# The last quarter of x on ScalarE's load queue, and 36 warm-up products instead of 39

## The chip, the cores and the metric

The kernel runs on one core of one Trainium2 chip. A core has five engines, which each run their own list of instructions: TensorE (PE, with its weight loads as PEld), VectorE (DVE), ScalarE (ACT), GpSimd (POOL) and SyncE (SP). They wait for each other, and for loads from memory (DMA), by semaphores. The metric is the device time of one execution in microseconds (us), lower is better.

## The reference

Two blocks of a hybrid transformer, on 256 latent tokens and 256 context tokens of width 1024. Every sublayer has this form, where `mod` comes from the condition `c` by a product with `mod_w`:

```python
def _rms(t, g):
    y = t32 * lax.rsqrt(jnp.mean(t32 * t32, axis=-1, keepdims=True) + NORM_EPS)
    return y.astype(t.dtype) * g

def _modulate(t, g, shift, scale):
    return _rms(t, g) * (1 + scale) + shift

lat = lat + 0.5 * mod[:, 0, 2] * _swiglu(_modulate(lat, norm_g[i, 0], mod[:, 0, 0], mod[:, 0, 1]), ffn_w13[i, 0], ffn_w2[i, 0])
```

Block 0 is a feed-forward layer, a short convolution and a second feed-forward layer, on both streams; block 1 has attention with two key heads in the middle and leaves the latent stream alone at its end. What concerns the change is the very first step: the root mean square over the 1024 channels of the input, for 512 tokens.

## The kernel before

The tokens of both streams stand side by side: `x` is one tile of 128 partitions by 8 channel groups by 512 tokens (256 latent, 256 context), 2 MB in all. Weights come in pieces of 512 KB, and each is split into a rounded part (`wh`, ScalarE, line 108) and the rest (`wl`, VectorE, line 109); a product is made of three products of such parts (lines 137 to 139). The loads of `x` and of nearly all weights are issued by SP, the constants by ScalarE's queue.

The start, with the lines of the profile:

```python
    def cload(key, shape, eng=None):                                    # 72
        t = const.tile(list(shape), F32, name=key, tag=key)
        (eng or nc.scalar).dma_start(t, a[key])                         # 74
        return t

    ccol = cload("ccol", [P, KT, 2])                                    # 78
    x = act.tile([P, KT, T2], F32, name="x", tag="x")
    for q in range(4):
        nc.sync.dma_start(x[:, 2 * q : 2 * q + 2, :], a["xT"][:, 2 * q : 2 * q + 2, :])   # 81
    modb = cload("modb", [P, 2, 72])                                    # 82
    normg = cload("normg", [P, 2, 3, KT])
    ident = cload("ident", [P, P])
```

After that ScalarE makes SiLU of the condition (`sccol`, line 96, from `ccol`) and issues the small load `rowsum`. Then the first stage runs:

- `square_add(k)` for k = 0 to 7, in that order: ScalarE squares channel group k of `x` (`sq`, line 258, out of three buffers in turn); VectorE copies (line 264, k = 0) or adds (line 266, k = 1 to 6) the two halves into `acc`, one for the latent tokens and one for the context tokens. The last square goes to TensorE as it is. One quarter of `x` holds two channel groups.
- `sb1` (line 904): VectorE adds 1 to a part of `modb`. In VectorE's list it stands ahead of the first copy into `acc`.
- `fill(WARM)` (line 897): TensorE multiplies a tile of ones by itself, 39 times, into a tile `idle` that nothing reads. Each such product is two records of the profile.
- `rms_sum` (line 275): TensorE sums `acc` and the last square over the partitions into `ss`; ScalarE takes the root (`rs`, line 280) and VectorE the reciprocal (`ri`, line 284); two products with `ident` (line 293) spread it over all partitions (`ris`, line 953).
- `mod_pe` and `mod_turn` (steps P and T): rows of the modulation, `pr`, from `pm` (loads at line 916) and `sccol` at line 926, turned by products with `rowsum` at line 938, and added to `sb1` or `modb` at line 943.
- `hr` (line 963) and `hh`, `hl` (lines 973 to 987): the normalized input, on which the first products with `w13` wait (line 1000, `pg` and `pu`).

The order within this stage is written out by hand (`FIRST_STEPS`, under a manual schedule for TensorE, VectorE, ScalarE and SP); elsewhere a scheduler orders the instructions when the program is built. Landings are told by eight semaphores that the loads take in turn: a load that takes a semaphore waits, on the engine that issues it, until the load before it on that semaphore has landed.

Of the kernel before, what the change touches and what calls it, by code (L numbers as in the profile page):

```python
# [9 lines left out]
F32 = mybir.dt.float32  # L10
# [6 lines left out]
P = 128  # L17
D = 1024
KT = D // P
S = 256  # L20
T2 = 2 * S
# [6 lines left out]
HEADS = 8  # L28
KVH = 2
EPS = 1e-6  # L30
WARM = 39
FILL = 5


# [13 lines left out]
def hybrid_kernel(ctx: ExitStack, tc: tile.TileContext, a: dict, out: bass.AP):  # L48
    nc = tc.nc
    const = ctx.enter_context(tc.tile_pool(name="const", bufs=1))  # L50
    wp = ctx.enter_context(tc.tile_pool(name="wp", bufs=2))
    act = ctx.enter_context(tc.tile_pool(name="act", bufs=1))
# [19 lines left out]
    def cload(key, shape, eng=None):  # L72
        t = const.tile(list(shape), F32, name=key, tag=key)
        (eng or nc.scalar).dma_start(t, a[key])
        return t


    ccol = cload("ccol", [P, KT, 2])
    x = act.tile([P, KT, T2], F32, name="x", tag="x")
    for q in range(4):  # L80
        nc.sync.dma_start(x[:, 2 * q : 2 * q + 2, :], a["xT"][:, 2 * q : 2 * q + 2, :])
    modb = cload("modb", [P, 2, 72])
    normg = cload("normg", [P, 2, 3, KT])
    ident = cload("ident", [P, P])
# [185 lines left out]
    def rms_sum(s, parts):  # L270

        pq = psmall("ss")
        for i in range(2):
            for n, t in enumerate(parts):
                nc.tensor.matmul(
                    pq[:, S + i : S + i + 1], t[:, i * P : i * P + P], ones[:, 0:1],
                    start=(n == 0), stop=(n == len(parts) - 1),
                )
        rs = tp.tile([P, 2], F32, name=nm("rs"), tag="rs")
        nc.scalar.activation(  # L280
            out=rs, in_=pq[:, S : S + 2], func=AF.Sqrt, scale=1.0 / D, bias=eps_t
        )
        ri = tp.tile([P, 2], F32, name=nm("ri"), tag="ri")
        nc.vector.reciprocal(ri, rs)
        return pq, ri
# [608 lines left out]
    def fill(n):  # L894

        for _ in range(n):
            nc.tensor.matmul(idle[:, :P], ones, ones, start=True, stop=True)
# [156 lines left out]
    with tc.manual_schedule(engines={e.engine for e in queues}):  # L1054
        fill(WARM)
        sums = [rms_sum(s, (accs[s], accs[s, "last"])) for s in range(2)]
# [429 lines left out]
```

## Time and profile before

| | |
|---|---|
| Time, median of 3 runs | 1567.11 us (1566.95 to 1568.15) |
| Profiled execution, its own time | 1566.27 us |
| Span of the profiled execution | 1564.5 us |
| TensorE busy | 1552.8 us (99% of the span) |
| VectorE busy | 1284.7 us (82%) |
| ScalarE busy | 775.2 us (50%) |
| Moved by DMA | 263.53 MB, mean 168 GB/s |
| DMA rate in the first 39 us | 370 GB/s |

The profile is one execution. A row of its timeline has the start, the length, the engine (with a q where the engine's sequencer only issues), the line, the operation, the tile written and the tiles read, the number of instructions, and in brackets how long the engine sat idle before and what ended that. A row of waits has who waited for whom, the sum in us, the number of waits and the longest. A row of the transfers has what is loaded, the issuing queue, the number, the size, and the median time from issue to landing. A row of a stretch has its bounds and length, then busy time and records of PE, PEld, DVE, ACT and POOL, the granted clock of TensorE, the DMA share and GB/s. TensorE's records overlap, so a busy TensorE is not one at its peak.

### The profile page before, as it was taken

To read this page: it belongs to the slowest core of one execution; us is meant where nothing else is said; L and a number is where in the kernel's file an instruction comes from. 1 tells how busy PE (TensorE), PEld (TensorE's weight loads), DVE (VectorE), ACT (ScalarE), POOL (GpSimd) and SP (SyncE) were. 2 spreads that over 40 slices of the span, in tenths; PEclk is the share of its full clock that TensorE was granted. 3 is DMA by queue.
4 is the path that set the end of the run, shared out by engine and by line. 5 is a ranking of instruction groups with operands and counts; after the bars stand their busy time and mean duration, and the time that the engine had idled before them with its cause. 6 is when DMAs were issued, how large, how long until landed. Compare 5 with 4: busy or idle time off the path is not lost.

```text
span 1564.5 us, 26382 instructions
## 1 busy us (share of the span) xinstructions
PE 1552.8 (99%) x10296; PEld 1422.4 (91%) x10296; DVE 1284.7 (82%) x2029; ACT 775.2 (50%) x1297; POOL 224.7 (14%) x188
## 2 busy tenths in 40 slices
PE   9999999999999999999999999999999999999999
PEld 7898998999888899989999899989999899898888
DVE  5789789889987588978978888978978788888676
ACT  5642453545323465436435475436445456674553
POOL 0012304100000111132131111131131002300000
PEclk9999999999999999999999999999999999999999
DMA  9567567564665525665665635665765743277562
GB/s 370 195 187 203 133 174 195 136 186 141 190 191 177 124 67 149 189 161 125 196 160 139 188 84 135 194 164 120 257 164 155 236 151 118 85 238 218 171 197 74
DMA packets 88254, 263.53 MB, mean 168 GB/s; under 512 B 10817, under 2 KB 12609, under 8 KB 88129
## 3 DMA queue, kind: packets, MB, share of 16 engines
q1 hardware_dynamic: 69408, 230.72, 46.1%
q0 software_dynamic: 16128, 29.37, 11.4%
q10 hardware_dynamic: 2592, 1.76, 0.4%
q8 instruction: 80, 1.31, 0.3%
q14 instruction: 46, 0.37, 0.1%
HBM read 259.45 MB, written 1.05 MB: 167 GB/s over the span
## 4 chain that ended last, share of the span: by engine, by line
PE 83%; DVE 9%; DMA 3%; ACT 2%; issue 2%; POOL 0%; POOLq 0%; DVEq 0%; ACTq 0%; SPq 0%
PE py L138 7%; PE py L137 7%; PE py L139 7%; PE p L137 6%; PE p L138 5%; PE p L139 5%; PE q L137 4%; PE q L139 4%; PE q L138 4%; DVE junk L178 2%; PE py L145 2%; PE pu L145 2%; PE pg L145 2%; DMA wr<-in_modT 2%; DVE wl L109 2%
## 5 line engine op out<-in xcount | busy, mean ns | idle before, releaser
L108 ACT ACTIVATE wh<-wr 128x1024 fp32r<-128x1024 f32 (+2 forms) x446 | 394.6, 913 | 329.6 <-PE py L138 123.3
L109 DVE TENSOR_TENSOR wl<-wr,wh 128x1024 fp32r<-128x1024 f32 (+2 forms) x446 | 459.0, 1053 | 91.6 <-ACT wh L108 73.0
L178 DVE CUSTOM_DVE_ANT_0 junk<-wr,scbc,modb 128x1024 bf16<-128x1024 f32 x213 | 275.0, 1291 | 49.3 <-DMA wr<-in_modT 46.8
L138 PE MATMUL py<-gl,wh 128*128 128x512 f32 (+1 forms) x570 | 213.4, 374 | 0.1
L137 PE MATMUL py<-gh,wh 128*128 128x512 f32 (+1 forms) x570 | 213.5, 375 | 0.0
L139 PE MATMUL py<-gh,wl 128*128 128x512 f32 (+1 forms) x570 | 213.0, 374 | 0.0
L704 POOL TENSOR_SCALAR wr<-wr 128x512 f32<-128x512 f32 x56 | 100.1, 1788 | 708.3 <-DMA wr<-in_w 474.4
L567 DVE SCALAR_TENSOR_TENSOR x<-py,mod,x 128x256 f32<-128x256 f32 x213 | 94.2, 478 | 51.8 <-PE py L139 40.8
L137 PE MATMUL p<-th,wh 128*128 128x256 f32 x448 | 126.8, 283 | 0.0
L138 PE MATMUL p<-tl,wh 128*128 128x256 f32 x448 | 126.8, 283 | 0.0
L139 PE MATMUL p<-th,wl 128*128 128x256 f32 x448 | 126.8, 283 | 0.0
L139 PEld LDWEIGHTS py<-gh,wl 128*128 128x128 f32 x570 | 107.3, 188 | 19.2
L138 PEld LDWEIGHTS py<-gl,wh 128*128 128x128 f32 x570 | 107.4, 188 | 18.5 <-DVE gl L109 0.5
L137 PEld LDWEIGHTS py<-gh,wh 128*128 128x128 f32 x570 | 107.4, 188 | 18.4
L115 POOL DMA_DIRECT2D w4l<-in_w x56 | 52.2, 932 | 283.2 <-ACT w4l L114 205.7
L137 PE MATMUL q<-bh,wh 128*128 128x256 f32 x320 | 90.9, 284 | 1.6 <-ACT wh L108 0.8
L139 PE MATMUL q<-bh,wl 128*128 128x256 f32 x320 | 90.9, 284 | 0.4 <-DVE wl L109 0.3
L138 PE MATMUL q<-bl,wh 128*128 128x256 f32 x320 | 90.5, 283 | 0.0
L138 PEld LDWEIGHTS p<-tl,wh 128*128 128x128 f32 x448 | 86.0, 192 | 0.3
L137 PEld LDWEIGHTS p<-th,wh 128*128 128x128 f32 x448 | 86.0, 192 | 0.3
L139 PEld LDWEIGHTS p<-th,wl 128*128 128x128 f32 x448 | 86.0, 192 | 0.0
L764 ACT ACTIVATE sg<-sg 128x512 f32<-128x512 f32 x56 | 35.4, 631 | 88.8 <-DVE sg L763 88.7
(304 smaller groups left out, 4081.2 us busy)
## 6 DMA issues: line engine op xcount, KB each, us to landing
wr<-in_w SPq DMA_DIRECT2D x120, 512.0 KB, 4.7
wr<-in_modT SPq DMA_DIRECT2D x117, 512.0 KB, 4.9
wr<-in_w2b SPq DMA_DIRECT2D x64, 448.0 KB, 4.1
wr<-in_w2a SPq DMA_DIRECT2D x32, 512.0 KB, 4.8
wr<-in_w SPq DMA_DIRECT2D x56, 256.0 KB, 3.5
wr<-in_w POOLq DMA_DIRECT2D x56, 256.0 KB, 4.7
w4l<-in_w POOLq DMA_DIRECT2D x56, 256.0 KB, 6.1
pm<-in_mod SPq DMA_DIRECT2D x16, 512.0 KB, 10.4
```

The costliest lines, as they stand in the source:

```text
L108: nc.scalar.activation(out=hi, in_=src, func=AF.Copy)
L109: return nc.vector.tensor_tensor(out=lo, in0=src, in1=hi.bitcast(F32), op=ALU.subtract)
L115: nc.gpsimd.dma_start(out=lo, in_=src, accum_op=ALU.add)
L137: nc.tensor.matmul(ps, wh, mh, start=first, stop=False, **kw)
L138: nc.tensor.matmul(ps, wh, ml, start=False, stop=False, **kw)
L139: nc.tensor.matmul(ps, wl, mh, start=False, stop=last, **kw)
L145: nc.tensor.matmul(ps, w[0], m[2], start=first and n == 0, stop=False)
L178: nc.vector.tensor_tensor_reduce(out=junk, in0=raw, in1=scbc[:, v, :], scale=0.5 if ch in (2, 8) else 1.0, scalar=modb[:, l, col : col + 1 ...
L567: ins = nc.vector.scalar_tensor_tensor(out=x[:, m, s * S : s * S + S], in0=ps[:, o : o + S], scalar=g[:, m, s : s + 1], in1=x[:, m, s * S ...
L704: nc.gpsimd.tensor_scalar(out=r1[:, :T2], in0=r2[:, :T2], scalar1=-1.0, scalar2=None, op0=ALU.mult)
L764: nc.scalar.activation(out=self.sg, in_=self.sg, func=AF.Silu)
```

## The change

The last quarter of `x` (channel groups 6 and 7) is loaded by ScalarE's queue, the other three by SP's. In ScalarE's list this load stands behind `ccol` and ahead of `modb`, `normg` and `ident`; the loop over the quarters runs 0, 3, 1, 2. The squares are still made in the order of the channel groups. The first stage has 36 fill products instead of 39. The order of all other instructions is the same on every engine. The semaphores of the first loads change with the order: the second load of `pm` now takes the one of the last quarter, the fourth load of `pm` that of `modb`, and `rowsum` that of the first quarter.

```diff
-WARM = 39
+WARM = 36
...
+    x = act.tile([P, KT, T2], F32, name="x", tag="x")
     ccol = cload("ccol", [P, KT, 2])
-    x = act.tile([P, KT, T2], F32, name="x", tag="x")
-    for q in range(4):
-        nc.sync.dma_start(x[:, 2 * q : 2 * q + 2, :], a["xT"][:, 2 * q : 2 * q + 2, :])
+    for q in (0, 3, 1, 2):
+        eng = nc.scalar if q == 3 else nc.sync
+        eng.dma_start(x[:, 2 * q : 2 * q + 2, :], a["xT"][:, 2 * q : 2 * q + 2, :])
     modb = cload("modb", [P, 2, 72])
     normg = cload("normg", [P, 2, 3, KT])
     ident = cload("ident", [P, P])
```

Lines behind the changed loop move by one: line 904 becomes 905, and so on.

## The prediction

> **What bounds the kernel now.** I read the page first, then, because the edit touches only the loads at the very start, the chain of waits, the timeline and the transfers of the first 20 us.
>
> ```profile
> span 1564.5 us, 26382 instructions
> PE 1552.8 (99%) x10296; PEld 1422.4 (91%) x10296; DVE 1284.7 (82%) x2029; ACT 775.2 (50%) x1297; POOL 224.7 (14%) x188
> PE 83%; DVE 9%; DMA 3%; ACT 2%; issue 2%; POOL 0%; POOLq 0%; DVEq 0%; ACTq 0%; SPq 0%
> ```
>
> TensorE (PE) is the bound: 83% of the chain that ended last, DMA 3%. So a shift of TensorE's first useful product moves the end by about as much, unless something later takes it up. The chain of waits in order of time opens like this (start, length, what):
>
> ```profile
> 1.05 11.07 PE idle L897 x78
> 12.12 1.68 PE ss L275 x16
> 13.80 1.00 PE pr L926 x16
> 14.80 1.09 PE ss L293 x8
> 15.91 1.07 PE pr L926 x16
> 16.98 1.16 PE pr L938 x8
> 18.23 0.17 DVE mod L943
> 18.42 1.10 ACT hh L973 x2
> ```
>
> The chain first runs through the fill products (39 products are 78 records), then the norm's sums `ss`, the modulation rows `pr`, and the first normalized tile `hh`. By this row nothing but the fills holds `ss` back. The timeline says how far the data were ahead of them:
>
> ```profile
> 0.74 0.42 ACTq L74 DMA_DIRECT2D ccol<-in_ccol  x1
> 1.17 0.42 SPq L81 DMA_DIRECT2D x<-in_xT  x1
> 1.19 0.44 ACTq L74 DMA_DIRECT2D modb<-in_modb  x1
> 4.84 0.33 SPq L81 DMA_DIRECT2D x<-in_xT  x1
> 6.24 0.17 DVE L904 TENSOR_SCALAR sb<-modb 128x8 f32<-128x8 f32 x1 [4.96 <-DMA modb<-in_modb]
> 6.32 0.49 DVE L264 COPY acc<-sq 128x256 f32<-128x256 f32 x2
> 6.73 3.44 DVE L266 TENSOR_TENSOR acc<-acc,sq 128x256 f32<-128x256 f32 x10
> 10.12 1.15 ACT L258 ACTIVATE sq<-x 128x512 f32<-128x512 f32 x2 [1.24 <-DMA x<-in_xT]
> 10.78 0.76 DVE L266 TENSOR_TENSOR acc<-acc,sq 128x256 f32<-128x256 f32 x2 [0.61 <-ACT sq L258]
> 11.96 0.28 PE L275 MATMUL ss<-ones,acc 128*128 128x1 f32 x2
> ```
>
> The last quarter of `x` lands at about 10.1, its squares end at 11.27, and VectorE's (DVE's) last two additions end at 11.54; the first `acc` is done one addition earlier, near 11.2, and `ss` starts at 11.96. So the fills end some 0.7 us after the data.
>
> The row to keep in mind is the one at 6.24: VectorE waits 4.96 us for `modb` before it may start the first accumulation, because `sb1` stands ahead of the accumulations in its list. From `modb` on it has 2 copies and 12 additions and runs them nearly without a break: copies 0.08 us after `sb`, additions 0.49 after it, and 10 additions in 3.44 us, so about 0.34 us each once pipelined. Then it waits 0.61 us for a square.
>
> **The loads.** `x` comes as four pieces of 512 KB, here 1 to 4 in channel order. First, in four narrow windows of the transfers, issue to landing (last figure); then SyncE's (SP's) wait; then four stretches of 1 us, with TensorE's records first (x6, x9, x11, x11) and GB/s last:
>
> ```profile
> x<-in_xT SPq DMA_DIRECT2D x1, 512.0 KB, 3.9
> ccol<-in_ccol ACTq DMA_DIRECT2D x1, 8.0 KB, 4.1
> ...
> x<-in_xT SPq DMA_DIRECT2D x1, 512.0 KB, 4.9
> modb<-in_modb ACTq DMA_DIRECT2D x1, 72.0 KB, 5.0
> ...
> x<-in_xT SPq DMA_DIRECT2D x1, 512.0 KB, 5.9
> normg<-in_normg ACTq DMA_DIRECT2D x1, 24.0 KB, 6.1
> ...
> x<-in_xT SPq DMA_DIRECT2D x1, 512.0 KB, 5.2
> ```
> ```profile
> SPq L81 <- DMA ccol<-in_ccol: 2.8, 1, 2.8
> ```
> ```profile
> 4.00:5.00 1.00, 1.00 (x6) 1.00 (x6) 0.00 (x0) 0.52 (x3) 0.00 (x0) 1.00 1.03 410
> 5.00:6.00 1.00, 1.00 (x9) 1.00 (x8) 0.00 (x0) 0.81 (x3) 0.00 (x0) 1.00 1.04 403
> 6.00:7.00 1.00, 1.00 (x11) 1.00 (x11) 0.76 (x4) 1.00 (x3) 0.00 (x0) 1.00 1.21 372
> 7.00:8.00 1.00, 1.00 (x11) 1.00 (x11) 1.00 (x4) 0.87 (x2) 0.00 (x0) 1.00 0.79 263
> ```
>
> Two things are seen. First, an 8 KB constant takes as long (4.1) as the 512 KB piece issued beside it (3.9), 72 KB as long (5.0) as the second piece (4.9), 24 KB (6.1) as the third (5.9): ScalarE's (ACT's) queue advances transfer by transfer in step with SP's. Second, SP could issue the fourth piece only at 4.84, after 2.8 us of waiting for `ccol`, whose landing semaphore it reuses; the rate sags to 263 GB/s at 7 to 8 us.
>
> **The change part by part.** *The fourth piece on ACT's queue.* It goes out behind `ccol` at about 1.2 instead of 4.84, and the hole at 7 to 8 us closes. ACT's list gets one issue longer (0.4 us, the `modb` row) ahead of an activation that waits for `ccol` anyway, so that costs nothing. In step, as the rows show, the order of landing is: piece 1 with `ccol`, at 0.73 + 3.9 = 4.6; then piece 2 with piece 4; then piece 3 with `modb`; then the first `pm` with `normg`; then the second `pm` with `ident`. At 410 GB/s a 512 KB piece is 1.28 us, so pieces 2 and 4 together land near 4.7 + 2.6 = 7.3 (estimate). Piece 3 with `modb` needs about 1.4 more (pieces 1 to 2: 4.6 to 6.1), so the last piece lands near 8.7, 1.4 us earlier than now, but `modb` near 8.9 instead of 6.2. `ident` comes near 11.7 (estimate: two more such steps), ahead of its use at L293; `rowsum` is needed later still.
>
> *What this does to the squares and sums.* ACT still squares in channel order, and piece 3 is now the last. After 8.7 there are four squares left instead of two. But VectorE is later than that: `sb1` waits for `modb`, and behind it in VectorE's list stand both copies and all twelve additions; TensorE's `ss` waits for them, and ACT's squares too, since only three buffers hold squares. From 8.9: additions start 0.5 later at 9.4; the first `acc`'s last addition is the eleventh, ten steps of 0.34 on, and takes about 0.4: 9.4 + 3.4 + 0.4 = 13.2. `ss` starts then at about 13.25 instead of 11.96: **+1.3 us**.
>
> *Three fills fewer.* Warm records come at 11 per us (row 6 to 7), so six records are 0.55 us. The fills would end near 11.4. As `ss` now waits for VectorE, this saves nothing; it opens an idle gap of about 1.9 us on TensorE.
>
> *The rest.* SP's next loads follow with no hole, each a little over 1 us earlier than now. Does an earlier weight pay the delay back? The first split of `w13`:
>
> ```profile
> 17.70 0.63 ACT L108 ACTIVATE wh<-wr 128x512 fp32r<-128x512 f32 x1 [0.24 <-DMA wr<-in_w]
> 18.42 0.60 ACT L973 ACTIVATE hh<-hr,mod,A 128x256 fp32r<-128x256 f32 x1
> ```
>
> It waited 0.24 us for its data and ended at 18.33, while `mod` ended at 18.40: both held `hh`, and `mod` hangs on `ss`. So an earlier weight gives nothing, and a later `ss` moves `hh` in full. All further instruction orders are the same in both programs, so I carry +1.3 us to the end.
>
> Bounds for that term: if `modb` landed as now, `ss` would be free at 11.2 to 11.4, −0.6 us; if the step of pieces 2 and 4 were as slow as the fourth piece now (5.2 against 3.9 for the first, 1.3 us more), +2.6. I take +1.3, which rests on the three pairs of landing rows.
>
> *A rule that speaks against the change.* The Trainium skill, "DMA: Bandwidth & Descriptors", section "Issuing engines are not separate DMA queues", says that loads from several engines end on the same 16 DMA engines and only save issue time. By it the fourth piece gains nothing but its earlier issue. The rows agree in rate (410 GB/s with one big queue), but here the issue time saved is 2.8 us of waiting. The same page, section "Queues, rings and completion order", says that each DMA engine alternates between queues packet by packet; the pairs of landing rows are what that would look like.
>
> **The sum.** The profiled execution took 1566.27 us (span 1564.5), 0.84 under the median of 1567.11. 1566.27 + 1.3 = 1567.6. Of the 0.84 some belongs to the fills: they run at 6 records per us until about 5.5 us and at 11 after it, and if that step comes 1 us later they end 0.45 us later, which binds before and no longer after. I take 0.6 of it along: **1568.2 us**, 0.07% over the median. A measurement of this kernel can tell about 0.2%, or 3.1 us, from no change.
>
> **The rivals.**
> *Data come early and the fills were the bound (chance 0.12).* If ACT's queue does not hold `modb` behind the fourth piece, `ss` starts when 36 fills end, −0.6 us: 1566.5. For it: `ss` starts directly at the fills' end today. Against it: the landing rows go in pairs.
> *The clock falls back in the new gap (0.20).* Mechanism: after the last fill TensorE idles from 11.4 to 13.2 and then has only one-column products until about 15. The fill rows show what a slow clock means: 6 records per us against 11, and it took from 1.05 to about 5.5 to come up (the granted clock column says 1.00 all through, so it does not show this step). A relapse of that length, 4.4 us, costs 4.4 × (1 − 6/11) = 2.0 us; two cost 4.0. With the +1.3 that is 1570.2 or 1572.2: slower. It decides if the monitor looks at a stretch that is mostly idle. Against it: the gap of 1.9 us is short, and the stretch from 12 to 18 with its small products keeps the fast clock today. The Trainium skill, "TensorE: Matmul & The Clock Gate", Part 1, puts the window at about 3.4 us, free-running, and asks for an idle window; by that a gap of 1.9 us is too short, and no run here shows a longer one inside the kernel.
> *The shift is taken up later or the landing order differs (0.06):* no change, 1567.1.
>
> **How the numbers follow.** My forecast has 0.62, with a range of its own from 1567.0 to 1569.5 (the bounds 0 to +2.6 us with the offset). The range for 8 in 10, 1566.2 to 1570.6, reaches to the first rival below and to one relapse above; two relapses and surprises are left out. Slower by over 0.2% needs 1570.2: most of the second rival, 0.17. Faster by over 0.2% needs 3.1 us, which no part of the change holds: 0.03. Within: 0.80.
>
> **What would show it.** Right: `sb` on VectorE ends its wait for `modb` at 8 to 9.5; ACT waits for `x` before its third and fifth squares; `ss` starts at 12.8 to 13.8, released by `acc`, with TensorE idle before it; SP's wait for `ccol` now stands before `pm`; `hh` near 19.7. Wrong: `modb` landing near 6, `ss` at the end of the fills, or fill and `pr` records at 6 per us again after 11 us.

## The result, and the profile after

The changed kernel takes 1570.57 us in the median of 22 runs (1565.83 to 1575.54), against 1566.67 us (1564.02 to 1568.91, 22 runs) for the kernel before: a ratio of 1.0025, with a 95% interval from 1.0017 to 1.0032. So it is slower by about 3.9 us. The profiled execution took 1569.65 us (span 1567.9).

The chain of waits of the changed kernel opens thus (start, length, what):

```profile
1.67 7.84 DMA modb<-in_modb
9.53 0.17 DVE sb L905
10.01 0.48 DVE acc L267 x2
...
13.37 0.43 DVE acc L267
13.84 3.09 PE ss L276 x16
16.93 1.86 PE pr L927 x16
18.80 2.01 PE ss L294 x8
20.80 1.22 PE pr L927 x16
23.28 0.17 DVE mod L944
23.48 0.60 ACT hh L974
```

The fills have left the chain. It now runs through the load of `modb`, the addition `sb`, and the accumulations behind it. But look at the lengths too: `ss` takes 3.09 us where it took 1.68, the first `pr` 1.86 where it took 1.00, the spreading of the root 2.01 where it took 1.09. From `ss` to `hh` it is 9.6 us where it was 6.5. The timeline shows the same start:

```profile
1.05 9.77 PE L898 MATMUL idle<-ones 128*128 128x128 f32 x72 [1.05 <-DVE eps_t L89]
7.88 0.63 ACT L259 ACTIVATE sq<-x 128x512 f32<-128x512 f32 x1 [1.25 <-DMA x<-in_xT]
9.53 0.17 DVE L905 TENSOR_SCALAR sb<-modb 128x8 f32<-128x8 f32 x1 [8.25 <-DMA modb<-in_modb]
10.01 4.11 DVE L267 TENSOR_TENSOR acc<-acc,sq 128x256 f32<-128x256 f32 x12
10.20 3.31 ACT L259 ACTIVATE sq<-x 128x512 f32<-128x512 f32 x5 [1.69 <-DVE acc L265]
13.84 0.38 PE L276 MATMUL ss<-ones,acc 128*128 128x1 f32 x2 [3.02 <-DVE acc L267]
```

VectorE waits 8.25 us for `modb` and then makes all twelve additions in one go; ScalarE's fourth square waits 1.69 us for a buffer that VectorE still reads; TensorE idles 3.02 us between the last fill and `ss`. Issue to landing, in narrow windows of the transfers:

```profile
x<-in_xT SPq DMA_DIRECT2D x1, 512.0 KB, 4.1
ccol<-in_ccol ACTq DMA_DIRECT2D x1, 8.0 KB, 4.2
...
x<-in_xT SPq DMA_DIRECT2D x1, 512.0 KB, 6.7
x<-in_xT ACTq DMA_DIRECT2D x1, 512.0 KB, 6.9
...
x<-in_xT SPq DMA_DIRECT2D x1, 512.0 KB, 7.7
modb<-in_modb ACTq DMA_DIRECT2D x1, 72.0 KB, 7.8
```

The pairs have changed as the edit says: the second quarter now keeps step with the last one (6.7 and 6.9), and `modb` with the third (7.7 and 7.8). Last, the stretches, where the third figure from the end is TensorE's granted clock:

```profile
4.00:5.00 1.00, 1.00 (x10) 1.00 (x10) 0.00 (x0) 1.00 (x1) 0.00 (x0) 1.00 1.05 374
11.00:14.00 3.00, 0.16 (x2) 0.16 (x2) 3.00 (x10) 2.85 (x5) 0.00 (x0) 1.00 0.91 296
14.00:15.00 1.00, 1.00 (x8) 1.00 (x8) 0.12 (x1) 0.80 (x1) 0.00 (x0) 0.70 0.89 336
15.00:19.00 4.00, 4.00 (x27) 2.71 (x27) 0.33 (x2) 0.62 (x3) 0.00 (x0) 0.50 1.03 412
19.00:21.00 2.00, 2.00 (x12) 1.71 (x16) 0.48 (x1) 0.81 (x3) 0.00 (x0) 0.50 1.01 412
21.00:22.00 1.00, 1.00 (x17) 0.33 (x9) 0.76 (x2) 0.21 (x1) 0.00 (x0) 0.89 1.03 418
```

The kernel before had the full clock there:

```profile
15.00:19.00 4.00, 3.98 (x41) 3.13 (x41) 2.60 (x7) 2.61 (x7) 0.00 (x0) 1.00 1.00 363
```

Soon after the idle stretch the clock falls: 0.70 between 14 and 15 means a fall at 14.4, and 0.89 between 21 and 22 a return at 21.2. For 6.8 us the granted clock was half of the full one. This is the rule, not this one execution: the mean granted clock was below 1.000 in 19 of the 22 runs of the change. Those nineteen took 1570.9 us in the mean, the other three 1567.4.

### The profile page after: what moved, and what is told of

Same layout as the page of the kernel before. It is cut to its first block, busy times and chain, and to the rows that moved or that the text cites. A ratio compares the mean times of both kernels' runs of the same rounds, so it can differ in the third digit from the quotient of the medians.

```text
span 1567.9 us, 26370 instructions
## 1 busy us (share of the span) xinstructions
PE 1553.3 (99%) x10290; PEld 1423.0 (91%) x10290; DVE 1286.4 (82%) x2029; ACT 775.8 (49%) x1297; POOL 225.5 (14%) x188
## 4 chain that ended last, share of the span: by engine, by line
PE 89%; DVE 5%; DMA 2%; ACT 2%; issue 1%; POOL 0%; POOLq 0%; ACTq 0%; DVEq 0%; SPq 0%
PE py L139 9%; PE py L138 9%; PE py L140 9%; PE p L138 6%; PE p L139 6%; PE p L140 6%; PE q L138 5%; PE q L140 5%; PE q L139 5%; PE py L146 2%; PE pu L146 2%; PE pg L146 2%; PE py L148 1%; PE pg L148 1%; PE pu L148 1%; PE pv L138 1%
## 5 line engine op out<-in xcount | busy, mean ns | idle before, releaser
L138 PEld LDWEIGHTS py<-gh,wh 128*128 128x128 f32 x570 | 107.4, 188 | 18.4
L735 DVE TENSOR_TENSOR wr<-wr,wr 128x1024 f32<-128x1024 f32 x56 | 69.1, 1233 | 9.2 <-ACT w4h L114 7.9
```

The costliest lines, as they stand in the source:

```text
L138: nc.tensor.matmul(ps, wh, mh, start=first, stop=False, **kw)
L735: tt(out=v(r2), in0=v(r2), in1=s2.unsqueeze(1).to_broadcast([P, 2, T2]), op=ALU.subtract,)
```

## The experiments

Two questions: what makes `ss` late, and is the fall of the clock caused by the gap? Theory A: `modb` lands late behind 512 KB, VectorE's list stands behind it, and the gap that this opens on TensorE brings the slow clock. Every ratio is to the kernel before on the same chip. Starts of `ss` and `hh`, and the time that TensorE idles ahead of `ss` (the gap), are from each kernel's one profiled execution. "Slow clock" counts the runs with a mean granted clock below 1.000; the kernel before was run on three more chips along with the others. The mean does not say where in a run the clock was low. In the four profiles that have it (the change, 39 fills, 24 fills, `sb1` later) the only such stretch lies between 12 and 22 us.

| kernel | ratio (95% interval) | `ss`, `hh` (us) | gap (us) | slow clock |
|---|---|---|---|---|
| before | 1 | 11.96, 18.42 | none | 8 of 35, 7 of 35, 3 of 21 |
| the change | 1.0025 (1.0017 to 1.0032) | 13.84, 23.48 | 3.02 | 19 of 22 |
| change, 39 fills | 1.0017 (1.0008 to 1.0026) | 13.69, 21.74 | 1.25 | 10 of 12 |
| change, 46 fills | 1.0006 (0.9996 to 1.0015) | 13.76, 20.24 | none | 1 of 12 |
| before, 36 fills | 1.0002 (0.9991 to 1.0013) | 11.46, 18.48 | 0.1 | 3 of 12 |
| before, 24 fills | 1.0004 (0.9994 to 1.0013) | 11.29, 20.95 | 2.44 | 11 of 11 |
| change, `modb` ahead of the quarter | 1.0000 (0.9989 to 1.0011) | 11.78, 18.35 | 0.1 | 1 of 11 |
| change, `sb1` later | 0.9998 (0.9989 to 1.0007) | 11.76, 19.81 | 0.90 | 5 of 11 |
| landing order | 1.0002 (0.9993 to 1.0012) | 11.63, 18.45 | none | 1 of 11 |
| quarter behind the constants, 32 fills | 0.9989 (0.9979 to 0.9998) | 10.60, 17.26 | 0.1 | 2 of 11 |
| the same, a second time | 0.9995 (0.9986 to 1.0004) | 10.51, 17.08 | 0.72 | 1 of 11 |
| quarter behind the constants, 36 fills | 1.0005 (0.9995 to 1.0015) | 12.14, 18.60 | none | 1 of 11 |

**The gap filled: 46 fills.**

```diff
-WARM = 36
+WARM = 46
```

> The changed kernel with 46 fill products instead of 36, all else equal: the fills then end at about 13.4 us, where the sums ss become free. Theory A (the loss is modb's late landing, +1.9 us at ss, and on top of it the slow clock that follows the idle gap): modb still lands near 9.5 and ss starts near 13.9, but the clock does not fall back, the mean granted clock is 1.000, ss to hh takes 6.5 us as in the kernel before instead of 9.6; time about 1568.5, that is +1.9 over before and 2 under the change. Rival B (the clock falls back for another reason, such as the one-column sums coming later, not for the gap): slow stretch and time as in the change, about +3.9.

```profile
1.04 12.88 PE idle L898 x92
13.93 1.69 PE ss L276 x16
16.62 1.09 PE ss L294 x8
20.04 0.17 DVE mod L944
20.24 1.10 ACT hh L974 x2
```

`modb` and `ss` are as late as in the change, but the sums take 1.69 and the spreading 1.09 us again, and the slow clock is gone from all but one run. Ten more useless products bring the time from 1.0025 to 1.0006. This is A in kind; the remaining loss, about 1 us with an interval that still holds none, is less than the 1.9 us expected.

**The loads alone: 39 fills.**

```diff
-WARM = 36
+WARM = 39
```

> The changed loads with 39 fill products as before. Theory A (late modb plus the idle gap): ss still starts near 13.8, released by the accumulations; the gap before it is 0.6 us shorter than in the change, so fewer or shorter slow stretches: mean loss between that of the kernel with 46 fills (+1.0 in the mean) and that of the change (+3.8), about +2.5 us. Rival B (the three fills are beside the point, the gap does not set the clock): +3.8 as in the change.

```profile
13.69 0.38 PE L276 MATMUL ss<-ones,acc 128*128 128x1 f32 x2 [1.25 <-DVE acc L267]
```

`ss` is as late, behind a gap of 1.25 us here. The loss, 2.7 us by the ratio, lies between the other two, as A has it, and this profile has 3.4 us at half clock (16.4 to 19.8) where the change has 6.8. But the interval overlaps that of the change, and 10 of 12 runs have the slow clock, much the same share as 19 of 22. That the three fills matter here is likely, not shown; against 46 fills the intervals overlap too, while the counts of the slow clock (10 of 12, 1 of 12) are far apart.

**The fills alone: the loads before, 36 fills.**

```diff
-WARM = 39
+WARM = 36
```

> The loads of the kernel before with 36 fill products. Theory A: the fills end near 11.2, where the first accumulation is done, no gap of note; ss 0.3 to 0.7 us earlier, the clock as before, time 0 to 0.7 us under before, which is not to be told from it. Rival F (the 36 fills alone bring the slow clock): slow stretches in most runs and +1.5 or more.

```profile
9.13 8.73 DMA wr<-in_w
18.51 1.07 ACT hh L973 x2
```

Nothing to be told from the kernel before. By themselves the three fills cost nothing that could be seen. A gain of up to 0.7 us did not show either: the chain ahead of `hh` goes through the first weight of `w13` there, which lands at 17.9, and no longer through the fills.

**The gap alone: the loads before, 24 fills.**

```diff
-WARM = 39
+WARM = 24
```

> The kernel before with 24 fill products instead of 39 and its loads unchanged: the data of ss are ready at about 11.3, the fills end near 8.5, an idle gap of 2 to 3 us as in the change but without any late landing. Theory A (an idle gap of this length brings the slow clock): ss near 11.3, a stretch at 0.5 of one or two windows of 3.4 us in most runs, mean granted clock 0.998 to 0.999, time +1 to +3 over before in spite of an ss that is 0.6 us earlier. Rival B (the gap does not matter): mean clock 1.000, time 0 to 0.6 us under before.

```profile
11.29 0.38 PE L275 MATMUL ss<-ones,acc 128*128 128x1 f32 x2 [2.44 <-DVE acc L266]
```
```profile
12.00:13.00 1.00, 1.00 (x9) 1.00 (x9) 0.10 (x1) 0.86 (x2) 0.00 (x0) 0.74 1.02 418
13.00:19.00 6.00, 6.00 (x44) 3.69 (x44) 1.60 (x6) 1.38 (x4) 0.00 (x0) 0.50 1.04 415
19.00:20.00 1.00, 1.00 (x12) 0.52 (x4) 0.40 (x1) 0.39 (x2) 0.00 (x0) 0.85 0.99 393
```

With no load changed, a gap of 2.44 us makes the clock fall, at 12.5, and come back at 19.3; in all eleven runs the mean clock was below 1.000. The gap is enough. It is the gap and not the small number of fills: with 32 fills and a gap of at most 0.7 us (below) 2 and 1 of 11 runs have the slow clock. The time moved less than A said: `hh` came 2.5 us later, but the ratio is 1.0004, with an interval from −0.9 to +2.0 us. How much of it arrives at the end is open (below).

**`modb` ahead of the quarter.**

```diff
+    modb = cload("modb", [P, 2, 72])
     for q in (0, 3, 1, 2):
         eng = nc.scalar if q == 3 else nc.sync
         eng.dma_start(x[:, 2 * q : 2 * q + 2, :], a["xT"][:, 2 * q : 2 * q + 2, :])
-    modb = cload("modb", [P, 2, 72])
```

> The changed kernel with modb ahead of the last quarter of x in ScalarE's list, all else equal (36 fills). Theory A: the loss is modb's place behind 512 KB. modb lands near 6.3, the last x near 9.3, ss starts at the end of the fills or at about 11.5, the clock stays; time 0.3 to 0.8 us under before. Rival C (sharing of the two queues slows x itself, so that the sums are late whatever modb does): ss at 13 or later, time as in the change, +3 or more.

```profile
6.11 0.17 DVE L905 TENSOR_SCALAR sb<-modb 128x8 f32<-128x8 f32 x1 [4.83 <-DMA modb<-in_modb]
9.30 2.19 ACT L259 ACTIVATE sq<-x 128x512 f32<-128x512 f32 x4 [1.90 <-DMA x<-in_xT]
9.96 2.10 DVE L267 TENSOR_TENSOR acc<-acc,sq 128x256 f32<-128x256 f32 x6 [1.27 <-ACT sq L259]
```

One line moved up takes back the whole loss. But there is no gain: `x` is complete at 9.3 instead of 10.0, yet four squares and six additions stand behind it instead of two and two, and `ss` starts at 11.78.

**`sb1` out of the way.**

```diff
         sums = [rms_sum(s, (accs[s], accs[s, "last"])) for s in range(2)]
+        nc.vector.tensor_scalar(out=sb1, in0=modb[:, 0, KT : 2 * KT], scalar1=1.0, ...)
```

(and its old place left empty)

> The changed kernel with the addition that makes sb1 from modb placed behind the two reciprocals in VectorE's list, all else equal: modb still lands near 9.5. Theory A (modb costs only because VectorE's whole list of copies and additions stands behind it): the accumulations start near 6.1 again, the end of the last x (9.3) and the four squares behind it set ss, at about 11.6; no or little slow clock; time within 0.5 us of before. Rival D (the squares are what is late, ScalarE having four left after 9.3, and sb1 is beside the point): ss stays near 13.8 and time near +3.9.

```profile
9.28 2.19 ACT L259 ACTIVATE sq<-x 128x512 f32<-128x512 f32 x4 [0.74 <-DMA x<-in_xT]
11.76 0.38 PE L276 MATMUL ss<-ones,acc 128*128 128x1 f32 x2 [0.90 <-DVE acc L267]
14.12 0.15 DVE L1055 TENSOR_SCALAR sb<-modb 128x8 f32<-128x8 f32 x1
```

`modb` is as late as in the change, and no longer matters: `ss` at 11.76, the time as before. So the late landing costs only through the list that stands behind `sb1`. The four squares and the additions behind them are the limit here too. In the profiled execution the clock fell (14.5 to 17.9) after a gap of only 0.90 us; 5 of 11 runs have the slow clock, and what gap the others had is not known.

**Squares in the order of landing.** The channel groups are squared in the order 0 to 3, 6, 7, 4, 5, with `sb1` later and 34 fills.

```diff
-    for k in range(KT):
-        square_add(k, 0, T2)
+    for n, k in enumerate((0, 1, 2, 3, 6, 7, 4, 5)):
+        square_add(k, 0, T2, n)
```

> The changed loads, with sb1 behind the reciprocals, the channel groups squared and added in the order in which they land (0 to 3, 6, 7, 4, 5) and 34 fill products; the sum is that of the same eight squares. Theory A (what is left is the four squares behind the last landing): ss starts at 10.6 to 11.0, little slow clock, time 0.5 to 1.3 us under before. Rival G (the stage is held by something behind ss, a load or the modulation rows): ss earlier, but hh not before 18.0, time as before.

```profile
9.57 8.01 DMA wr<-in_w
18.45 1.10 ACT hh L972 x2
```

A miss for A, and what rival G expected. The last addition started at 10.8, but in the profiled execution the 34 fills held `ss` until 11.6, as their rate had come up only near 7 us. And an earlier `ss` would have helped little: the chain ahead of `hh` runs through the first weight of `w13`, which landed at 17.6, and TensorE waited for a load of `pm` before its later `pr` rows, until 16.4. The time is that of before.

**The quarter behind the constants.** Squares and `sb1` as in the change, 32 fills.

```diff
-    for q in (0, 3, 1, 2):
-        eng = nc.scalar if q == 3 else nc.sync
-        eng.dma_start(x[:, 2 * q : 2 * q + 2, :], a["xT"][:, 2 * q : 2 * q + 2, :])
+    for q in range(3):
+        nc.sync.dma_start(x[:, 2 * q : 2 * q + 2, :], a["xT"][:, 2 * q : 2 * q + 2, :])
     modb = cload("modb", [P, 2, 72])
     normg = cload("normg", [P, 2, 3, KT])
     ident = cload("ident", [P, P])
+    nc.scalar.dma_start(x[:, 6:8, :], a["xT"][:, 6:8, :])
```

> The last quarter of x on ScalarE's queue behind ccol, modb, normg and ident instead of ahead of them, sb1 in its old place, squares in channel order, 32 fill products. Theory A (it is the place ahead of modb that costs, not the queue): modb lands near 6.2, the last quarter near 9 and is the last one again, two squares behind it; ss near 10.3 to 10.8; time 0.5 to 1.5 us under before unless the slow clock comes oftener. Rival C (two big loads side by side slow the whole start): the last quarter not before 10, ss not before 11.5, time as before or above.

```profile
6.29 0.17 DVE L905 TENSOR_SCALAR sb<-modb 128x8 f32<-128x8 f32 x1 [5.01 <-DMA modb<-in_modb]
9.33 1.15 ACT L259 ACTIVATE sq<-x 128x512 f32<-128x512 f32 x2 [0.41 <-DMA x<-in_xT]
17.26 1.09 ACT L974 ACTIVATE hh<-hr,mod,A 128x256 fp32r<-128x256 f32 x2 [0.20 <-DVE mod L944]
```

Everything that the change was short of is here: the last quarter starts early, the constants do not wait for it, and it lands last, with two squares behind it. `hh` starts 1.2 us earlier than before. Not all of that is the earlier `ss`: the chain ahead of `hh` runs through the first weight of `w13` here, which landed at 16.4 instead of 17.7. The same kernel, a second time:

> The same kernel as the one with the last quarter behind the constants and 32 fills, a second time on another occasion: if its gain is real, ss near 10.6 and a time 1 to 2.5 us under before; if it was chance, within 0.7 us of before.

The first ratio excludes no change, the second (0.9995, from 0.9986 to 1.0004) does not; both profiles show `hh` at 17.1 to 17.3. The second gain, 0.8 us by the ratio, lies between the two expectations. If there is a gain, it is small and about what the profile allows; it is not settled. With 36 fills, so that only the place in the queue, and with it the turn of the semaphores, differs from the change:

> The last quarter of x on ScalarE's queue behind the constants, with 36 fill products as in the change, so that the place in the queue is the only difference from it. Theory A (the place ahead of modb is the whole cause, by late sums and by the gap that they open): modb near 6.2, ss at the end of the fills, 11.0 to 11.6, clock as before, time 0 to 1.3 us under before, that is 4 or more under the change. Rival H (part of the loss comes from elsewhere in the change): 1 us or more over before.

```profile
1.04 11.26 PE idle L898 x72
12.30 1.68 PE ss L276 x16
18.60 1.10 ACT hh L974 x2
```

The place in the queue is the cause: 1.0005 against 1.0025, intervals apart. It was no faster than before, though, and the row gives a likely reason: in this execution the same 72 records of fills took 11.26 us, where the change's took 9.77.

## Why the prediction was right or wrong

**The late `modb`: right in kind, too small.** The pairs of landing rows gave the order in which the loads would come, and up to `modb` it came so; `normg` then landed at 9.8, 1.1 us ahead of the first `pm` that I had paired it with. Pieces 2 and 4 side by side took longer than I reckoned at 410 GB/s: they landed at 7.9 and 8.1, not 7.3, and `modb` at 9.5, not 8.9. `ss` started at 13.84, +1.9 us and not +1.3. From `modb` to `ss` I had 4.35 us, and it took 4.33.

**The last piece earlier: right, and worth nothing, as forecast.** It landed at 9.3 for 8.7 forecast. That four squares then hold `ss` to 11.8 even without `modb` in the way is what the two kernels with `modb` first and with `sb1` later show.

**The weights: right that they pay nothing back, wrong on when they come.** `mod` ended 0.03 us before `hh` started in the change. But SP's next loads were not a little over 1 us earlier: the first `wr` was issued at 9.89 instead of 8.61 and landed at 18.4 instead of 17.7. SP waited 2.7 us for the last quarter of `x`, whose semaphore the second load of `pm` now takes, a wait that the prediction left out. It stayed hidden behind the late `ss`.

**The slow clock: the step that failed.** I put it at 0.20 and outside the sum, and it was the larger part of the loss. I weighed one figure, a gap of 1.9 us, against the length of a window; the gap was 3.0 us, for two reasons. `ss` was 0.6 us later. And the fills ended at 10.8 and not 11.4, because their end depends on when their rate steps up, which I used for the offset to the median but not for the gap. Moreover gaps of 0.9 and 1.25 us were enough in other profiled executions, while one of 0.72 us (the quarter behind the constants, second time) went by without a fall. What exactly the condition is stays open. In each of the four profiles with a fall, the 3.4 us before it held at most 0.8 us of products other than the one-column sums (an estimate from the timelines; with `sb1` later 0.7 us idle, 1.95 us of sums, 0.8 us of `pr`). That such sums hardly count as work that keeps the clock fits this, but no run tests it by itself. The price of a slow stretch was right, its length (4.4 us) was not: by the formula of the prediction, 5/11 of the stretch, 6.8 us cost 3.1 and 3.4 us cost 1.5. Measured between `ss` and `hh` it was 3.1 us for 6.8 (9.64 against 6.57 with `modb` first) and 1.5 for 3.4 (8.05 with `sb1` later).

The Trainium skill, "TensorE: Matmul & The Clock Gate", Part 1, asks for an idle window of about 3.4 us before the clock falls, and on that I had leaned. The lengths agree with it: one stretch of 3.4 us, or two. The condition does not: the clock fell after gaps of 3.0, 2.4, 1.25 and 0.9 us in the profiled executions, so here the measurement decides.

The sign of being wrong that the prediction named came too: 16 records of `pr` took 1.86 us after 11 us, where they took 1.00 before, and `hh` stood at 23.48, not near 19.7.

**The sum.** 1568.2 was the likeliest value, with 1567.0 to 1569.5 of its own; 1570.57 lies above that, and inside the range by 0.03 us. That is luck: the range's end was set for one relapse on top of +1.3 us, and what came in the profile was +1.9 us at `ss` and 6.8 us at half clock, 5.1 us at `hh`, of which 3.9 us are in the time. Forecast within 0.2% of before, it came out slower by 0.25%: the side of the second rival. By the kernel with 46 fills, which has the late `ss` without the slow clock, about 1 of the 3.9 us is the late `ss` and the rest the clock. The three runs of the change at a mean clock of 1.000 agree: 1567.4 us in the mean, less than 1 us over the kernel before. Each of these is uncertain by a microsecond or more.

**Carried in full to the end: not settled.** `hh` was 5.1 us late in the profile and the span 3.4 us longer; with 24 fills `hh` was 2.5 us late and the ratio is 1.0004. A straight line through the eleven rows of the table below the first gives about 0.7 us of time for 1 us of `hh` (an estimate, from one profile each). For 24 fills it gives 1.7 us, which their interval still holds; so the two do not contradict each other. With runs of one kernel lying up to 5 us apart (1564.02 to 1568.91 for the kernel before), two profiles cannot tell what is given back later from what differs between executions.

## What to carry to other kernels

Before a big load is put into a queue, look at what small loads stand behind it there, and at what in-order engine has its list standing behind those: 72 KB late by 3.3 us held two copies and twelve additions. A wait that opens a gap on TensorE at the start can cost more by the clock than by itself, so where the first real product is late, the fills have to reach up to it. Move the transfer that is needed last to a second queue, but behind that queue's constants, and keep it the last one that is used; here that took the loss away, and whether it gains is not settled.

## What the runs showed of the hardware

The two queues went on nearly in step in the first three pairs of loads: a 72 KB load landed 0.1 to 0.2 us after the 512 KB piece that it was paired with, before (5.0 and 4.9 us) and after (7.8 and 7.7). It is no strict rule: in the change the 24 KB of `normg` landed 0.3 us after `modb` and 1.1 us ahead of the next 512 KB.

The time at which the fills' rate steps up, from 6 or 7 records per us to 11 or 12, differs between executions, and with it the end of a fixed number of fills. The granted clock reads 1.00 throughout, so that the step is the clock's is inferred from the rate. 72 records took 9.77 us with 10 of them between 4 and 5 us (the change), and 11.26 us where the profile has 6 there:

```profile
4.00:5.00 1.00, 1.00 (x6) 1.00 (x6) 0.00 (x0) 0.99 (x2) 0.00 (x0) 1.00 1.03 406
5.00:6.00 1.00, 1.00 (x7) 1.00 (x6) 0.00 (x0) 0.71 (x3) 0.00 (x0) 1.00 1.02 388
```

(the kernel with the quarter behind the constants and 36 fills). One program shows it as well: with the quarter behind the constants, 64 records took 9.48 us in one profile and 8.74 us in the other. A fixed number of fills can therefore be too short in one execution and too long in another. The slow clock came in stretches of 3.4 or 6.8 us in the four profiles that have it. In the kernel before, 18 of 91 runs had a mean clock below 1.000, but no profile of such a run shows where.
